# Scheduling priority for VectorE's operations of a state chain, and the distances 8, 10, 8 within a chunk

## The chip, the core and the metric

The kernel runs on one core of one Trainium2 chip. The metric is the device time of one execution in microseconds (us), the median of several runs. Five engines work side by side, each through its own queue in order: TensorE (PE: matmuls; PEld is its weight load), VectorE (DVE), ScalarE (ACT), GpSimd (POOL) and SyncE (SP, which only issues DMAs here).

## What is computed

A decoder block over 512 tokens of width 2048: a sliding-window attention branch and a gated DeltaNet branch from one normalised input, merged by gates, a projection and a last norm. The change touches the recurrence of the second branch, which runs over 8 chunks of 64 tokens for each of 32 value heads:

```
def step(state, inp):
    q_i, k_i, u_i, w_i, g_i, qk_i = inp
    v_new = u_i - w_i @ state
    o = (q_i * exp(g_i)) @ state + qk_i @ v_new
    k_dec = k_i * exp(g_last - g_i)
    state = state * exp(g_last) + k_dec^T @ v_new
    return state, o
```

## The kernel before

All matrix products with weights are done in float32 accuracy by splitting each operand into a rounded high part and the rest: `proj` takes two halves of a weight tile, and for each half `mm_half` gives PE eight matmuls high by high (L174), eight high by low (L176) and eight low by high (L179), 128x512 each. So a projection has 48 such matmuls. ACT makes the high part of a weight (L162); in the stage of the change GpSimd makes the low part (L165, two operations of 128x512 for each half).

PE's order is written out by the program. Everything else that PE must do is a generator (a job) in a `Flow`. After each matmul of a projection, `flow.tick()` counts all waiting jobs down by one, and a job that is due puts its next PE instructions at this place. `yield n` therefore means: n projection matmuls later. The orders on DVE, ACT and GpSimd are made by a scheduler, which takes among the operations that are ready, by its own account of time, the one of the best priority. Priority is by default the order of the program. Each engine then runs its list strictly in order.

In the stage of the change one head kh of 16 (a key head with its two value heads, h = 0 and 1) takes four projections, 192 matmuls: two value tiles and two gate tiles. After heads 3, 7 and 11 (`GATE_KH`) a fifth projection is put in, and at the end of the stage four more stand. Beside these run, as jobs: the causal convolution of a value tile (`conv`: three DVE operations L297 on the tile cy, after one on ACT), its transposes to tokens (`to_tokens`, vb, L538 and L539), the preparation of the keys of the next head (`prepare`: transposes L519, ktl by L523 and L525), the scan of a head (`scan`), and the output of a head (`finish`: L608 sums squares, eleven small operations L610 and L193 to L197 on 128x8 make a reciprocal root by Newton steps, L612 scales the whole output by it).

The scan is a serial chain through PE and DVE. For a chunk c it has four links:

- X (L555): PE multiplies the state `sn`; DVE makes `rr` of it (L561, one for each h), ACT makes xq.
- Y (L573): PE multiplies `rr`, DVE makes `sv` in three operations (L576 on both h, then L579 for each h), and `o` (L582), which isn't in the chain.
- SU (L588, L589): PE multiplies `sv`.
- DVE makes the new state `sn` (L594, one for each h; for the first chunk the copy L597, here called the seed).

The distances in matmuls are X to Y 8, Y to SU 8, SU to the next X 10. In the first chunk, which has no X, Y follows its start by 4. The scans of the heads stand in a queue of their own (`scans`), one behind the other; a scan of 8 chunks takes 194 matmuls.

Of the kernel before, what the change touches and what calls it, by code (L numbers as in the profile page):

```python
# [8 lines left out]
F32 = mybir.dt.float32  # L9
# [3 lines left out]
ALU = mybir.AluOpType  # L13
AX = mybir.AxisListType

P = 128
# [63 lines left out]
def hybrid_block(  # L80
# [21 lines left out]
    pe, dve, act, pool = nc.tensor, nc.vector, nc.scalar, nc.gpsimd  # L102
# [16 lines left out]
    def bank(tag, bufs=1):  # L119
        return ps.tile([P, S], F32, name=tag, bufs=bufs)  # L120
# [95 lines left out]
    eSuf = cst.tile([P, NT, 32], F32, name="eSuf")  # L216
    nbeG = cst.tile([P, NT, 32], F32, name="nbeG")
    vbe = cst.tile([P, NT, 32], F32, name="vbe")
    cq = cst.tile([P, NT, NK], F32, name="cq")
    eTot = [cst.tile([P, NT, 32], F32, name=f"eTot{p}") for p in range(2)]  # L220
# [265 lines left out]
    with ExitStack() as st:  # L486
# [58 lines left out]
        def scan(kh, vb, zs):  # L545
            slab, tq, kth, ktl = got.pop(kh)
            o = pv.tile([P, NT, 2, P], F32, name="o")
            s_cur = None
            v2 = slice(2 * kh, 2 * kh + 2)
            for c in range(8):  # L550
                T, p = divmod(c, 2)
                rk, rq = (H0, H1) if p == 0 else (H1, H0)
                if c:
                    xp = bank("pa").rearrange("p (h e) -> p h e", h=4)[:, 0:2, :]
                    pe.matmul(xp, slab[:, T, 2 * p:2 * p + 2, :].rearrange("d b i -> d (b i)"), s_cur,  # L555
                              start=True, stop=True)
                    rr = rrs[p]
                    xq = pv.tile([P, 2, P], F32, name="xq")
                    for h in range(2):
                        vh = 2 * kh + h  # L560
                        dve.scalar_tensor_tensor(rr[rk, h, :], xp[rk, h, :], nbeG[rk, T, vh:vh + 1], vb[rk, T, h, :],  # L561
                                                 ALU.mult, ALU.add)
                    for h in range(2):
                        vh = 2 * kh + h
                        act.activation(xq[rq, h, :], xp[rq, h, :], AF.Copy, scale=eGs[rq, T, vh:vh + 1])  # L565
                    yield 8
                else:
                    rr = rrs[p]
                    act.copy(rr[rk], vb[rk, T])
                    yield 4  # L570
                yp = bank("pb").rearrange("p (h e) -> p h e", h=4)[:, 0:2, :]
                for h in range(2):
                    pe.matmul(yp[:, h, :], tq[:, h * 4 + T, :], rr[:, h, :], start=True, stop=True)  # L573
                if c < 7:
                    sv = pv.tile([P, 2, P], F32R, name="sv")
                    dve.tensor_tensor(sv[rk], yp[rk], eSuf[rk, T, v2].unsqueeze(2).broadcast_to([64, 2, P]), ALU.mult)  # L576
                    for h in range(2):
                        vh = 2 * kh + h
                        dve.scalar_tensor_tensor(sv[rq, h, :], yp[rk, h, :], eSuf[rk, T, vh:vh + 1],  # L579
                                                 sv[rk, h, :].bitcast(F32), ALU.mult, ALU.subtract)  # L580
                if c:
                    dve.tensor_tensor(o[rq, T], xq[rq], yp[rq], ALU.add)  # L582
                else:
                    act.copy(o[rq, T], yp[rq])
                yield 8
                if c < 7:
                    su = bank("pc").rearrange("p (h e) -> p h e", h=4)[:, 0:2, :]
                    pe.matmul(su, kth[:, T, p, :], sv, start=True, stop=False)  # L588
                    pe.matmul(su, ktl[:, T, p, :], sv, start=False, stop=True)  # L589
                    s_new = pv.tile([P, 2, P], F32, name="sn")  # L590
                    if c:
                        for h in range(2):
                            vh = 2 * kh + h
                            dve.scalar_tensor_tensor(s_new[:, h, :], s_cur[:, h, :], eTot[p][:, T, vh:vh + 1],  # L594
                                                     su[:, h, :], ALU.mult, ALU.add)
                    else:
                        dve.tensor_copy(s_new, su)  # L597
                    s_cur = s_new
                    yield 10
            flow.start(finish(kh, o, zs))  # L600

        def finish(kh, o, zs):
            osq = pv.tile([P, NT * 2, P], F32, name="osq", bufs=1)
            ov = o.rearrange("p t h e -> p (t h) e")
            act.activation(osq, ov, AF.Square)
            so = pv.tile([P, 8], F32, name="so")
            ro = pv.tile([P, 8], F32, name="ro")
            dve.tensor_reduce(so, osq, AX.X, ALU.add)  # L608
            so4 = so.rearrange("p (t h) -> p t h", h=2)
            dve.scalar_tensor_tensor(so4, so4, 1.0 / P, cq[:, :, kh:kh + 1].broadcast_to([P, NT, 2]), ALU.mult, ALU.add)  # L610
            rsqrt(pv, ro, so, 8)
            dve.tensor_tensor(ov, ov, ro.unsqueeze(2).broadcast_to([P, 8, P]), ALU.mult)  # L612
            yield 36
            for h in range(2):
                tp = bank("tr", 2)
                for T in range(NT):
                    pe.transpose(tp[:, T * P:(T + 1) * P], o[:, T, h, :], ident)
                od = pv.tile([P, S], F32, name="od")
                tv = tp.rearrange("p (t c i) -> p t c i", t=NT, c=2)
                dv = od.rearrange("p (t c i) -> p t c i", t=NT, c=2)  # L620
                zv = zs[:, h, :].rearrange("p (t c i) -> p t c i", t=NT, c=2)
                for p in range(2):
                    dve.scalar_tensor_tensor(dv[:, :, p, :], tv[:, :, 1 - p, :], dnw, zv[:, :, p, :], ALU.mult, ALU.mult)
                nc.sync.dma_start(od_d[KT + 2 * kh + h], od)
                yield 6
# [4 lines left out]
        for kh in range(NK):  # L630
            vb = pv.tile([P, NT, 2, P], F32, name="vb")
            zs = pv.tile([P, 2, S], F32, name="zs", bufs=3)
            flow.start(prepare(kh), 24 if kh else 60)
            for h in range(2):
                vh = 2 * kh + h

                def then(acc):
                    y = conv(acc, 32 + vh, pv)
                    act.activation(y, y, AF.Silu)
                    after = (lambda kh=kh, vb=vb, zs=zs: scans.add(scan(kh, vb, zs))) if h else None  # L640
                    flow.start(to_tokens(y, vb, h, vh, after))

                proj(w_in[T_DN + 32 + vh], then)
            for h in range(2):
                proj(w_in[T_DZ + 2 * kh + h], lambda acc: act.activation(zs[:, h, :], acc, AF.Silu))
                if h == 0 and kh + 1 < NK:
                    load_head(kh + 1)
            if kh in GATE_KH:
                gate_tile(pv, 47 - n_gate)
                n_gate += 1  # L650
# [339 lines left out]
```

## Time and profile before

| what | value |
|---|---|
| median of 3 runs | 2933.49 us (2932.84 to 2934.3) |
| the profiled execution | 2932.62 us |
| its span in the profile | 2930.8 us |
| granted TensorE clock over the span | 0.997 of full speed |
| PE busy | 2848.7 us, 97% |
| DVE busy | 1766.8 us, 60% |
| ACT busy | 1028.7 us, 35% |
| GpSimd busy | 552.4 us, 19% |

Busy time is the time in which an engine has an instruction under way. The stage of the change lies between about 850 and 1850 us of the span. In a row of the timeline the first number is the start in us from the beginning of the span, the second the duration, x4 means that four equal instructions are merged, and the bracket at the end is the time that the engine stood idle before the instruction and what ended it.

### The profile page before, as it was taken

How to read it: one execution, taken by the hardware profiler on the slowest of the kernel's cores; microseconds unless marked ns; L12 is line 12 of the kernel's file. 1: busy time of each engine (PE TensorE's matmuls, PEld its weight loads, DVE VectorE, ACT ScalarE, POOL GpSimd, SP SyncE). 2: the span in 40 equal slices, each digit the busy share in tenths (PEclk: the TensorE clock that was granted, in tenths of full speed). 3: DMA queues.
4: the chain of work that ended last, by engine and by line, in shares of the span. 5: the costliest groups of instructions: out<-in, count | busy, mean ns of one | idle time of the engine just before them, and what ended most of it. 6: DMA issues, size and time to landing. Idle time of an engine off the chain costs nothing.

```text
span 2930.8 us, 36770 instructions
## 1 busy us (share of the span) xinstructions
PE 2848.7 (97%) x13594; PEld 2367.1 (81%) x13594; DVE 1766.8 (60%) x3520; ACT 1028.7 (35%) x1645; POOL 552.4 (19%) x464
## 2 busy tenths in 40 slices
PE   7999999999999999999999999999999999999998
PEld 7778888888887787788778778887788888888887
DVE  6686667979725555555555554378884455455434
ACT  5532222232333333334333333355553222222222
POOL 2410000000043333333333333023340000000010
PEclk9999999999999999999999999999999999999999
DMA  3344444353543333333333332423336554554533
GB/s 139 107 130 143 130 136 157 120 203 124 185 133 99 96 112 104 98 98 114 96 102 115 98 89 91 132 86 110 101 108 216 172 176 155 165 161 147 181 99 103
DMA packets 184627, 376.07 MB, mean 128 GB/s; under 512 B 65504, under 2 KB 82272, under 8 KB 183040
## 3 DMA queue, kind: packets, MB, share of 16 engines
q1 hardware_dynamic: 184448, 373.72, 40.7%
q8 instruction: 108, 1.77, 0.3%
q14 instruction: 71, 0.58, 0.1%
HBM read 316.97 MB, written 54.59 MB: 127 GB/s over the span
## 4 chain that ended last, share of the span: by engine, by line
PE 86%; DVE 10%; ACT 2%; issue 1%; POOL 0%; DMA 0%; SPq 0%; ACTq 0%; DVEq 0%
PE acc L179 24%; PE acc L176 23%; PE acc L174 23%; PE pa L555 2%; DVE cy L297 2%; PE pb L573 1%; PE fo L898 1%; PE fo L896 1%; PE fo L897 1%; PE acc L247 1%; PE tr L529 1%; DVE sv L579 1%; DVE ptl L760 1%; PE pc L588 1%; DVE ad L381 1%
## 5 line engine op out<-in xcount | busy, mean ns | idle before, releaser
L174 PE MATMUL acc<-hT_hi,whi 128*128 128x512 f32 x2592 | 1037.5, 400 | 0.0
L176 PE MATMUL acc<-hT_lo,whi 128*128 128x512 f32 x2592 | 1018.6, 393 | 0.0
L162 ACT CAST whi<-w 128x1024 fp32r<-128x1024 f32 x446 | 468.3, 1051 | 1183.4 <-PE acc L176 949.4
L179 PE MATMUL acc<-hT_hi,wlo 128*128 128x512 f32 x2592 | 685.6, 398 | 2.3 <-DVE wlo L165 2.3
L165 POOL TENSOR_TENSOR wlo<-w,whi 128x512 fp32r<-128x512 f32 x284 | 359.9, 1288 | 1283.6 <-PE acc L179 648.8
L165 DVE TENSOR_TENSOR wlo<-w,whi 128x512 fp32r<-128x512 f32 x608 | 423.3, 719 | 264.4 <-ACT whi L162 202.1
L176 PEld LDWEIGHTS acc<-hT_lo,whi 128*128 128x128 f32 x2592 | 488.7, 189 | 92.1
L174 PEld LDWEIGHTS acc<-hT_hi,whi 128*128 128x128 f32 x2592 | 488.4, 188 | 92.1
L179 PEld LDWEIGHTS acc<-hT_hi,wlo 128*128 128x128 f32 x2592 | 480.3, 188 | 99.0 <-DVE wlo L165 3.1
L174 PE MATMUL acc<-dh,whi 128*128 128x512 f32 x768 | 298.8, 389 | 0.0
L176 PE MATMUL acc<-dl,whi 128*128 128x512 f32 x768 | 298.8, 389 | 0.0
L179 PE MATMUL acc<-dh,wlo 128*128 128x512 f32 x768 | 189.7, 389 | 0.0
L561 DVE SCALAR_TENSOR_TENSOR rr<-pa,nbeG,vb 64x128 f32<-64x128 f32 x224 | 69.2, 348 | 183.8 <-PE pa L555 183.2
L297 DVE SCALAR_TENSOR_TENSOR cy<-acc,cw,cy 128x511 f32<-128x511 f32 (+2 forms) x192 | 142.8, 744 | 58.7 <-ACT cy L295 55.8
L859 DVE TENSOR_TENSOR gd<-acc,gl 128x512 f32<-128x512 f32 x80 | 55.2, 690 | 188.3 <-PE acc L179 188.3
L176 PEld LDWEIGHTS acc<-dl,whi 128*128 128x128 f32 x768 | 144.2, 188 | 30.0
L179 PEld LDWEIGHTS acc<-dh,wlo 128*128 128x128 f32 x768 | 144.1, 188 | 29.9
L174 PEld LDWEIGHTS acc<-dh,whi 128*128 128x128 f32 x768 | 144.1, 188 | 29.9
L916 POOL TENSOR_TENSOR y<-y,fw 128x512 f32<-128x512 f32 x12 | 18.9, 1609 | 658.7 <-ACT sqy L914 658.7
L576 DVE TENSOR_TENSOR sv<-pb,eSuf 64x256 fp32r<-64x256 f32 x112 | 46.9, 419 | 137.5 <-PE pb L573 137.3
L565 ACT ACTIVATE xq<-pa,eGs 64x128 f32<-64x128 f32 x224 | 69.0, 356 | 160.0 <-DVE rr L561 159.4
L467 DVE TENSOR_TENSOR m<-m,tm 128x62 f32<-128x62 f32 (+30 forms) x124 | 106.3, 857 | 2.8
(264 smaller groups left out, 3180.3 us busy)
## 6 DMA issues: line engine op xcount, KB each, us to landing
w<-w_in SPq DMA_DIRECT2D x326, 512.0 KB, 3.5
w<-w_dn SPq DMA_DIRECT2D x64, 512.0 KB, 3.5
gl<-ga_d SPq DMA_DIRECT2D x96, 256.0 KB, 2.6
w<-w_att SPq DMA_DIRECT2D x32, 512.0 KB, 3.9
w<-w_out SPq DMA_DIRECT2D x32, 512.0 KB, 3.5
of<-od_d SPq DMA_DIRECT2D x48, 256.0 KB, 4.0
kq_d<-slab SPq DMA_DIRECT2D x16, 512.0 KB, 2.8
ga_d<-gt SPq DMA_DIRECT2D x32, 256.0 KB, 3.0
```

Source lines behind the costliest of these rows:

```text
L162: act.copy(hi, w)
L165: lo_eng[0].tensor_sub(lo[:, r], w[:, r], hi[:, r].bitcast(F32))
L174: pe.matmul(acc, hi[:, k, :], rhi[k], start=first and k == 0, stop=False)
L176: pe.matmul(acc, hi[:, k, :], rlo[k], start=False, stop=False)
L179: pe.matmul(acc, lo[:, k, :], rhi[k], start=False, stop=last and k == n - 1)
L297: dve.scalar_tensor_tensor(y[:, sh:], acc[:, 0:S - sh], cw[:, t, 3 - sh:4 - sh], y[:, sh:], ALU.mult, ALU.add)
L467: dve.tensor_tensor(m[:, 0:jj, jj + 1:], m[:, 0:jj, jj + 1:], tm, ALU.add)
L555: pe.matmul(xp, slab[:, T, 2 * p:2 * p + 2, :].rearrange("d b i -> d (b i)"), s_cur, start=True, stop=True)
L561: dve.scalar_tensor_tensor(rr[rk, h, :], xp[rk, h, :], nbeG[rk, T, vh:vh + 1], vb[rk, T, h, :], ALU.mult, ALU.add)
L565: act.activation(xq[rq, h, :], xp[rq, h, :], AF.Copy, scale=eGs[rq, T, vh:vh + 1])
L576: dve.tensor_tensor(sv[rk], yp[rk], eSuf[rk, T, v2].unsqueeze(2).broadcast_to([64, 2, P]), ALU.mult)
L859: dve.tensor_tensor(gd, acc, gl, ALU.mult)
```

## The change

Three groups of DVE operations of the chain, those that make `rr`, `sv` and `sn`, are put into `with tc.high_priority()`: where one of them and another operation are ready together in the scheduler's account, the one of the chain is taken first. No operation is added or removed. The distances become X to Y 8, Y to SU 10, SU to X 8. The period of a chunk stays at 26 matmuls; in the last chunk, which has no SU, the end of the scan moves from 8 to 10 matmuls behind Y, so that a scan takes 196.

```
-                    for h in range(2):
-                        vh = 2 * kh + h
-                        dve.scalar_tensor_tensor(rr[rk, h, :], xp[rk, h, :], nbeG[rk, T, vh:vh + 1], vb[rk, T, h, :],
-                                                 ALU.mult, ALU.add)
+                    with tc.high_priority():
+                        for h in range(2):
+                            vh = 2 * kh + h
+                            dve.scalar_tensor_tensor(rr[rk, h, :], xp[rk, h, :], nbeG[rk, T, vh:vh + 1],
+                                                     vb[rk, T, h, :], ALU.mult, ALU.add)
...
-                    dve.tensor_tensor(sv[rk], yp[rk], eSuf[rk, T, v2].unsqueeze(2).broadcast_to([64, 2, P]), ALU.mult)
-                    for h in range(2):
-                        vh = 2 * kh + h
-                        dve.scalar_tensor_tensor(sv[rq, h, :], yp[rk, h, :], eSuf[rk, T, vh:vh + 1],
-                                                 sv[rk, h, :].bitcast(F32), ALU.mult, ALU.subtract)
+                    with tc.high_priority():
+                        dve.tensor_tensor(sv[rk], yp[rk], eSuf[rk, T, v2].unsqueeze(2).broadcast_to([64, 2, P]),
+                                          ALU.mult)
+                        for h in range(2):
...
-                yield 8
+                yield 10
                 if c < 7:
...
+                    with tc.high_priority():
+                        if c:
+                            for h in range(2):
...
+                        else:
+                            dve.tensor_copy(s_new, su)
                     s_cur = s_new
-                    yield 10
+                    yield 8
```

Three places of DVE's list show what this moves. The first is chunk 6 of head 4, where a convolution (cy) falls on the chain. Before:

```order
L561 SCALAR_TENSOR_TENSOR rr_6246<-pa,nbeG,vb 64x128 x2
L297 SCALAR_TENSOR_TENSOR cy<-acc,cw,cy 128x511
L576 TENSOR_TENSOR sv<-pb,eSuf 64x256
L297 SCALAR_TENSOR_TENSOR cy<-acc,cw,cy 128x510
L579 SCALAR_TENSOR_TENSOR sv<-pb,eSuf,sv 64x128
L297 SCALAR_TENSOR_TENSOR cy<-acc,cw,cy 128x509
L579 SCALAR_TENSOR_TENSOR sv<-pb,eSuf,sv 64x128
L582 TENSOR_TENSOR o<-xq,pb 64x256
```

The same place after the change (line numbers there are a little higher: L562 is rr, L578 and L582 are sv, L585 is o, L598 is sn):

```order
L562 SCALAR_TENSOR_TENSOR rr_6246<-pa,nbeG,vb 64x128 x2
L297 SCALAR_TENSOR_TENSOR cy<-acc,cw,cy 128x511
L578 TENSOR_TENSOR sv<-pb,eSuf 64x256
L297 SCALAR_TENSOR_TENSOR cy<-acc,cw,cy 128x510
L582 SCALAR_TENSOR_TENSOR sv<-pb,eSuf,sv 64x128 x2
L297 SCALAR_TENSOR_TENSOR cy<-acc,cw,cy 128x509
L598 SCALAR_TENSOR_TENSOR sn<-sn,eTot_100,pc 128x128 x2
L585 TENSOR_TENSOR o<-xq,pb 64x256
```

The two halves of sv now stand together; the third convolution has gone behind them, and one stays between L578 and L582.

The second place is the seed of head 6, from its sv on. Before, with the Newton steps (ro, nrt) and the scaling L612 of head 5's output around it:

```order
L579 SCALAR_TENSOR_TENSOR sv<-pb,eSuf,sv 64x128
L195 SCALAR_TENSOR_TENSOR nrt<-ro,so 128x8
L196 TENSOR_TENSOR nrt<-nrt,ro 128x8
L197 SCALAR_TENSOR_TENSOR ro<-nrt,ro 128x8
L195 SCALAR_TENSOR_TENSOR nrt<-ro,so 128x8
L196 TENSOR_TENSOR nrt<-nrt,ro 128x8
L597 COPY sn<-pc 128x256
L197 SCALAR_TENSOR_TENSOR ro<-nrt,ro 128x8
L612 TENSOR_TENSOR o<-o,ro 128x1024
```

The same place after (L616 is the scaling, L601 the seed):

```order
L582 SCALAR_TENSOR_TENSOR sv<-pb,eSuf,sv 64x128 x2
L196 TENSOR_TENSOR nrt<-nrt,ro 128x8
L197 SCALAR_TENSOR_TENSOR ro<-nrt,ro 128x8
L195 SCALAR_TENSOR_TENSOR nrt<-ro,so 128x8
L196 TENSOR_TENSOR nrt<-nrt,ro 128x8
L197 SCALAR_TENSOR_TENSOR ro<-nrt,ro 128x8
L616 TENSOR_TENSOR o<-o,ro 128x1024
L601 COPY sn<-pc 128x256
```

The seed has gone behind the last Newton step and the scaling. It is the same in head 7; in head 5 it stood behind the scaling before, too, and has two Newton steps between sv and the scaling now where there were three.

The third place is chunk 3 of head 6, where the keys of head 7 are prepared (ktl). Before:

```order
L576 TENSOR_TENSOR sv<-pb,eSuf 64x256
L579 SCALAR_TENSOR_TENSOR sv<-pb,eSuf,sv 64x128 x2
L582 TENSOR_TENSOR o<-xq,pb 64x256
L523 TENSOR_TENSOR ktl<-tr,kth 64x4x128
L525 CAST ktl<-ktl 64x4x128
L594 SCALAR_TENSOR_TENSOR sn<-sn,eTot_101,pc 128x128 x2
```

The same place after:

```order
L523 TENSOR_TENSOR ktl<-tr,kth 64x4x128
L525 CAST ktl<-ktl 64x4x128
L578 TENSOR_TENSOR sv<-pb,eSuf 64x256
L523 TENSOR_TENSOR ktl<-tr,kth 64x4x128
L582 SCALAR_TENSOR_TENSOR sv<-pb,eSuf,sv 64x128 x2
L585 TENSOR_TENSOR o<-xq,pb 64x256
```

Two operations of ktl now stand ahead of sv and one inside it. On PE the scan of head 6 stands 4 matmuls later than before, since the two scans ahead of it in the queue take 2 matmuls more each; so the four transposes L519, which stood right behind Y of this chunk, now stand four matmuls ahead of it.

## Rows read from the trace of the kernel before

**Rows 1.** Waits of PE, whole span: us in total, times, longest.
```profile
PE pc L588 <- DVE sv L579: 28.3, 27, 1.6
...
PE pa L555 <- DVE sn L597: 8.5, 8, 1.6
```
**Rows 2.** Waits of PE from 1098 to 1346 us, heads 4 to 7.
```profile
PE pc L588 <- DVE sv L579: 7.2, 7, 1.4
PE pa L555 <- DVE sn L597: 2.1, 2, 1.5
```
**Rows 3.** Timeline of PE, chunk 1 of head 4: Y, SU, X.
```profile
1112.26 0.61 PE L573 MATMUL pb<-rr,tq 128*128 128x128 f32 x4
...
1114.56 0.28 PE L588 MATMUL pc<-sv,kth 128*128 128x256 f32 x1
...
1117.07 0.59 PE L555 MATMUL pa<-sn,slabv 128*128 128x256 f32 x2
```
**Rows 4.** Timeline of DVE, the same chunk: sv, sn.
```profile
1112.91 0.43 DVE L576 TENSOR_TENSOR sv<-pb,eSuf 64x256 fp32r<-64x256 f32 x1 [1.67 <-PE pb L573]
1113.37 0.63 DVE L579 SCALAR_TENSOR_TENSOR sv<-pb,eSuf,sv 64x128 fp32r<-64x128 f32 x2
...
1114.99 0.61 DVE L594 SCALAR_TENSOR_TENSOR sn<-sn,eTot,pc 128x128 f32<-128x128 f32 x2 [0.55 <-PE pc L589]
```
**Rows 5.** Timeline of DVE, chunk 6 of head 4: convolution and sv.
```profile
1150.92 0.75 DVE L297 SCALAR_TENSOR_TENSOR cy<-acc,cw,cy 128x511 f32<-128x511 f32 x1 [1.51 <-ACT cy L295]
1151.59 0.40 DVE L576 TENSOR_TENSOR sv<-pb,eSuf 64x256 fp32r<-64x256 f32 x1
...
1152.68 0.34 DVE L579 SCALAR_TENSOR_TENSOR sv<-pb,eSuf,sv 64x128 fp32r<-64x128 f32 x1
...
1153.84 0.34 DVE L579 SCALAR_TENSOR_TENSOR sv<-pb,eSuf,sv 64x128 fp32r<-64x128 f32 x1
```
**Rows 6.** Timeline of PE, SU of this chunk.
```profile
1154.33 0.35 PE L588 MATMUL pc<-sv,kth 128*128 128x256 f32 x1 [1.41 <-DVE sv L579]
```
**Rows 7.** Timeline of DVE, head 5: Newton steps, scaling, seed.
```profile
1165.47 1.25 DVE L196 TENSOR_TENSOR nrt<-nrt,ro 128x8 f32<-128x8 f32 x1
...
1168.01 1.23 DVE L612 TENSOR_TENSOR o<-o,ro 128x1024 f32<-128x1024 f32 x1
1169.15 0.42 DVE L597 COPY sn<-pc 128x256 f32<-128x256 f32 x1
```
**Rows 8.** Timeline of PE, first X of head 5.
```profile
1169.62 0.70 PE L555 MATMUL pa<-sn,slabv 128*128 128x256 f32 x2 [1.54 <-DVE sn L597]
```
**Rows 9.** Timeline of GpSimd at this place.
```profile
1165.41 2.53 POOL L165 TENSOR_TENSOR wlo<-w,whi 128x512 fp32r<-128x512 f32 x2 [3.75 <-issue]
```
**Rows 10.** Timeline of DVE, head 6: a Newton step with GpSimd idle.
```profile
1229.30 0.17 DVE L197 SCALAR_TENSOR_TENSOR ro<-nrt,ro 128x8 f32<-128x8 f32 x1
```
**Rows 11.** Timeline of GpSimd, head 6.
```profile
1226.70 2.54 POOL L165 TENSOR_TENSOR wlo<-w,whi 128x512 fp32r<-128x512 f32 x2 [3.45 <-issue]
```
**Rows 12.** Timeline of PE, first X of head 6.
```profile
1230.25 0.70 PE L555 MATMUL pa<-sn,slabv 128*128 128x256 f32 x2 [0.57 <-DVE sn L597]
```
**Rows 13.** Timeline of PE, chunk 3 of head 6: Y and the keys' transposes.
```profile
1247.74 0.61 PE L573 MATMUL pb<-rr,tq 128*128 128x128 f32 x4
1248.19 0.60 PE L519 MATMUL tr<-ident,kc 128*128 128x128 f32 x4
```
**Rows 14.** Timeline of ACT there.
```profile
1248.82 0.58 ACT L522 CAST kth<-tr 64x512 fp32r<-64x512 f32 x1 [1.40 <-PE tr L519]
```
**Rows 15.** Timeline of GpSimd there.
```profile
1248.04 2.54 POOL L165 TENSOR_TENSOR wlo<-w,whi 128x512 fp32r<-128x512 f32 x2 [3.66 <-ACT xq L565]
```
**Rows 16.** Timeline of DVE, chunk 5 of head 7: ktl.
```profile
1322.52 0.68 DVE L523 TENSOR_TENSOR ktl<-tr,kth 64x512 fp32r<-64x512 f32 x1 [1.21 <-ACT kth L522]
1323.23 0.81 DVE L525 CAST ktl<-ktl 64x512 fp32r<-64x512 f32 x1
```
**Rows 17.** Timeline of GpSimd there.
```profile
1321.24 2.52 POOL L165 TENSOR_TENSOR wlo<-w,whi 128x512 fp32r<-128x512 f32 x2 [4.10 <-issue]
```

More of the change, by code (lines that the diff above doesn't have):

```diff
@@ L575, in scan @@
                     sv = pv.tile([P, 2, P], F32R, name="sv")
-                    dve.tensor_tensor(sv[rk], yp[rk], eSuf[rk, T, v2].unsqueeze(2).broadcast_to([64, 2, P]), ALU.mult)
-                    for h in range(2):
-                        vh = 2 * kh + h
-                        dve.scalar_tensor_tensor(sv[rq, h, :], yp[rk, h, :], eSuf[rk, T, vh:vh + 1],
-                                                 sv[rk, h, :].bitcast(F32), ALU.mult, ALU.subtract)
+                    with tc.high_priority():
+                        dve.tensor_tensor(sv[rk], yp[rk], eSuf[rk, T, v2].unsqueeze(2).broadcast_to([64, 2, P]),
+                                          ALU.mult)
+                        for h in range(2):
+                            vh = 2 * kh + h
+                            dve.scalar_tensor_tensor(sv[rq, h, :], yp[rk, h, :], eSuf[rk, T, vh:vh + 1],
+                                                     sv[rk, h, :].bitcast(F32), ALU.mult, ALU.subtract)
                 if c:
@@ L590, in scan @@
                     s_new = pv.tile([P, 2, P], F32, name="sn")
[L591 to L597, printed above, removed]
+                    with tc.high_priority():
+                        if c:
+                            for h in range(2):
+                                vh = 2 * kh + h
+                                dve.scalar_tensor_tensor(s_new[:, h, :], s_cur[:, h, :], eTot[p][:, T, vh:vh + 1],
+                                                         su[:, h, :], ALU.mult, ALU.add)
+                        else:
+                            dve.tensor_copy(s_new, su)
                     s_cur = s_new
-                    yield 10
+                    yield 8
             flow.start(finish(kh, o, zs))
```

## The prediction

> **What bounds the kernel now.** PE is busy for 97% of the span, in an order that the program writes out, and the change leaves the number of its matmuls as it is. So only time in which PE stands still can go or come. I read the waits of PE first. Over the whole span PE waits 28.3 us in 27 places at SU for sv and 8.5 us in 8 places at X for sn, 36.8 us together [rows 1]; these are the waits that the change can touch, and 36.8 us is the most that it can give. The same view by stretch says that they come back every four heads, the rhythm of the projection put in after heads 3, 7 and 11: heads 4 to 7 have 7.2 us in 7 places and 2.1 us in 2 [rows 2], 9.3 us, and four times this is 37.2 us (the last four heads have a little less). So I work out heads 4 to 7 and multiply.
>
> Then the timeline of a chunk with nothing else on DVE. Y starts at 1112.26, SU at 1114.56, X at 1117.07 [rows 3]; sv is ready at 1114.00 and sn at 1115.60 [rows 4]. SU starts 0.15 us after sv's end where it waits (1153.84 + 0.34, then 1154.33 [rows 5, 6]), so it could go at 1114.15: a slack of 0.41 us. For X the step is 0.05 us (1169.57, then 1169.62 [rows 7, 8]): it could go at 1115.65, a slack of 1.42 us. The lengths 2.30 us for 8 matmuls and 2.51 us for 10 give about 0.23 us for one, so two are 0.45 us. The link through sv is tight and waits when DVE does something else first; the link through sn waits only at the seed.
>
> **The distances.** Two matmuls more to SU, two less to X: slacks of 0.86 and 0.97 us in place of 0.41 and 1.42. Undisturbed chunks wait nowhere before and after. Where SU waits, 0.45 us goes. A scan takes 196 matmuls instead of 194 and a head has 192; so within four heads the second scan starts 2 later than now, the third 4, the fourth 6 (0.45, 0.91, 1.36 us), and the fifth projection takes it up again. At the end of the stage the last scan is 8 matmuls late, beside four projections of 48; this costs nothing, and without that cover 8 x 0.23 = 1.8 us.
>
> **The priority at the convolutions.** Chunk 6 of head 4: the first convolution is ready ahead of Y's result and stays first, L576 runs at 1151.59, the second convolution stays between, and the halves of sv then stand together. The first starts at 1152.68 as now, the two take 0.63 us [rows 4, 5], and sv ends at 1153.31, not 1154.18. SU may go at 1153.46; without its wait it would have come at 1154.33 - 1.41 = 1152.92 [rows 6] and now comes 0.45 us later, 1153.37. There remains 0.1 us of 1.41. The same addition for the four other places of this kind in heads 5 and 6, with their chains shifted, gives 0.1, 0.3 (two convolutions ahead of sv), 0 and 0.1 us. Together 0.6 us.
>
> **The priority at the keys.** In chunk 5 of head 7 ktl leaves sv free, and a wait goes whole. In chunk 3 of head 6 one comes. The transposes now start where Y started, 1247.74, and Y 0.45 us (the transposes' own time) and 0.91 us later, 1249.10 [rows 13]. ACT's copy starts 0.63 us behind the transposes and takes 0.58 [rows 13, 14], so L523 runs from 1248.95 to 1249.65. L525 then falls into GpSimd's pair of operations, which ends at 1250.58 [rows 15]. What that does is seen in head 7: there L525 took 0.81 us and ended at 1324.04, 0.28 us after GpSimd's pair (1323.76) [rows 16, 17]. So it ends at 1250.86, and behind it come L578 with 0.43, L523 with 0.69 and sv's halves with 0.63 us: 1252.6, SU at 1252.75. Due is 1249.10 + 2.30 + 0.45 = 1251.85. A new wait of 0.9 us.
>
> **The seeds.** Here the priority doesn't help. Head 5: after sv two Newton steps remain, and GpSimd's pair from 1165.41 to 1167.94 [rows 9] holds them: a step took 1.25 us inside the pair [rows 7], 0.17 us outside [rows 10]. The scaling starts at 1167.97, and X follows a scaling that stands ahead of the seed by 1169.62 - 1168.01 = 1.61 us [rows 7, 8]: 1169.58. Due is 1169.62 - 1.54 + 0.45 = 1168.53. The wait is 1.05 us in place of 1.54. Head 6: the pair ends at 1229.24 [rows 11] and holds two of five steps, three more take 0.2 us each with the gap, the scaling starts at 1229.9 and X at 1231.51; due is 1230.25 - 0.57 + 0.91 = 1230.59 [rows 12]. The wait is 0.9 us in place of 0.57. Head 7 has the same order; before, its wait was at SU, with a Newton step inside sv. I take 0.9 us. In head 4 the seed is free of Newton steps. Together 2.9 us.
>
> A rule bears on these two parts: the Trainium skill, "SBUF — State Buffer", section "SBUF: two separate sides", says that VectorE and GpSimd share a pair of SBUF ports as an exclusive lock, held for a whole instruction, and that the other side is blocked meanwhile. The trace agrees for L196 (1.25 against 0.17 us). By the rule the scaling, with two operands in SBUF, would be blocked too if it started inside a pair, which no run here shows; that makes a rival below.
>
> **The sum.** Heads 4 to 7 wait 0.6 + 0.9 + 2.9 = 4.4 us instead of 9.3. Four times 4.4 is 17.6 us against 36.8: 19.2 us go. The profiled execution took 2932.6 us, 0.9 us less than the median of the runs: 2913.4 us on its scale, 2914 us as a median. Everything else I take at nothing: no operation is added; ACT's copies for xq stand a place earlier or later between the casts of the weights, and in this stage the view of PE's waits names none for such a cast, only the two kinds of [rows 2].
>
> The bounds of what no row shows. GpSimd's pairs may stand elsewhere against the steps: without any overlap head 5's scaling would start at about 1166, and all seeds come in time (0 us); if each seed also waits for one more held step, 3 x 1.25 us come on top of 2.9. At the sv places the least is 0, and the most what they cost now, 6.2 us without the one that I count with head 7's seed. The new wait at the keys lies between 0 and 0.9 us. So four heads wait between 0 and 6.2 + 0.9 + 6.7 = 13.8 us, which is 2897 to 2952 us as a median, and I take 4.4, since each term comes from the row nearest to it.
>
> **Rivals.**
> - The waits go nearly whole: GpSimd's pairs slip past the Newton steps and the keys. For it: a held step depends on tenths of a us, and in the seed's neighbourhood the chain moves by 0.45 to 1.36 us. Against: GpSimd's place is tied to the projections, which keep theirs. What stays is about 1 us in four heads, 33 us go: 2900 us.
> - The waits only change places: chains shifted by 2, 4 and 6 matmuls meet other operations, as at the keys. Five more such waits of 0.9 us in four heads would eat the 4.9 us: 2932 us. Against it: in the new order nothing but one operation ever stands between the first and the other two operations of sv. For it: in two heads of four the seed has gone behind the scaling.
> - Slower: the scaling itself falls into GpSimd's pair and is held, with the seed and the whole chain behind it. The place is the seeds of the 12 heads that follow another without a fifth projection; the price is up to 2.5 us (a pair) each. The gain is gone from 19.2 / 12 = 1.6 us each on; at the full price 30 us come and 19 go: 2944 us. Against it: the Newton steps ahead of the scaling are held themselves until the pair ends, so that the scaling starts behind it [rows 7, 9].
> - The priority may not do what it says: at the seeds it doesn't, but at sv the order shows the halves together.
>
> **Chances.** The forecast 0.72, nearly whole 0.10, places changed 0.10, slower 0.06, something else 0.02. What a measurement of this kernel can tell from no change is about 0.2%, 5.9 us: faster means below 2927.6, which holds all of the first two and a little of the third; with its upper tail counted off, 0.84. Same 0.10, slower 0.06. The range: the forecast's own is 2.5 us to either side for four heads, 10 us in all, 2904 to 2924; to hold 8 in 10 with the rivals it reaches from 2902 to 2926.
>
> **What would show it.** SU's wait for sv falls from 28.3 us to about 6 to 10, most of it in two places of four heads (the keys in the third head, a seed); X's wait for the seed rises from 8.5 to about 11 or 12 us, in 12 places. L579's successor shows its two halves merged at the convolutions. DVE's busy time and PE's count of matmuls stay. I am wrong if the X waits are small (then GpSimd was elsewhere), if many new places of SU below 0.5 us appear, or if PE waits for casts of weights in the stage.

## The result and the profile after

| | us |
|---|---|
| predicted | 2914.0 (2902 to 2926) |
| after, median of 4 runs | 2914.12 (2912.18 to 2914.93) |
| before, beside it | 2933.32 (2932.84 to 2934.3) |
| ratio | 0.9933, 95% interval 0.9922 to 0.9945 |
| the profiled execution, span | 2914.18, 2912.4 |

The kernel became 19.2 us faster. The granted clock is 0.997 as before. The page's line of busy times is nearly that of before, so the time came out of PE's idle time. The two profiled executions differ by 18.4 us, which falls into two parts: from the first X to the end of the span 2069.4 us became 2048.5, 20.9 us less, while the first X started at 863.9 us instead of 861.4, 2.5 us later, after work that the change leaves alone.

```profile
PE 2850.0 (98%) x13594; PEld 2370.9 (81%) x13594; DVE 1762.9 (61%) x3520; ACT 1028.6 (35%) x1645; POOL 555.8 (19%) x464
```

The waits of PE over the whole span (us in total, times, longest), which answer to [rows 1]; L601 is the seed, L582 the halves of sv, L591 is SU:

```profile
PE pa L555 <- DVE sn L601: 13.2, 12, 1.5
...
PE pc L591 <- DVE sv L582: 4.2, 5, 1.2
```

28.3 + 8.5 = 36.8 us in 35 places became 13.2 + 4.2 = 17.4 us in 17. SU's wait for sv fell to a seventh, X's wait for the seed grew by a half. In heads 4 to 7 (1096 to 1342 us; [rows 2] before) the same view has 3.4 us in 3 places and 0.7 in one.

**The convolution.** VectorE's timeline in chunk 6 of head 4, which answers to [rows 5]: start, duration, operation, and in brackets the idle time before it.

```profile
1148.39 0.75 DVE L297 SCALAR_TENSOR_TENSOR cy<-acc,cw,cy 128x511 f32<-128x511 f32 x1 [1.50 <-ACT cy L295]
1149.06 0.40 DVE L578 TENSOR_TENSOR sv<-pb,eSuf 64x256 fp32r<-64x256 f32 x1
1149.39 0.73 DVE L297 SCALAR_TENSOR_TENSOR cy<-acc,cw,cy 128x510 f32<-128x510 f32 x1
1150.15 0.60 DVE L582 SCALAR_TENSOR_TENSOR sv<-pb,eSuf,sv 64x128 fp32r<-64x128 f32 x2
```

The halves of sv stand together and end at 1150.75; SU started at 1150.90 and had stood idle for 0.09 us by PE's records, in place of the 1.41 us of [rows 6].

**The keys.** Chunk 3 of head 6 on VectorE, on GpSimd and on PE ([rows 13 to 15] before):

```profile
1243.15 1.16 DVE L525 CAST ktl<-ktl 64x512 fp32r<-64x512 f32 x1
1244.34 0.43 DVE L578 TENSOR_TENSOR sv<-pb,eSuf 64x256 fp32r<-64x256 f32 x1
1244.69 0.69 DVE L523 TENSOR_TENSOR ktl<-tr,kth 64x512 fp32r<-64x512 f32 x1
1245.41 0.63 DVE L582 SCALAR_TENSOR_TENSOR sv<-pb,eSuf,sv 64x128 fp32r<-64x128 f32 x2
```
```profile
1241.48 2.54 POOL L165 TENSOR_TENSOR wlo<-w,whi 128x512 fp32r<-128x512 f32 x2 [4.09 <-issue]
```
```profile
1242.55 0.61 PE L574 MATMUL pb<-rr,tq 128*128 128x128 f32 x4
...
1245.05 0.39 PE L176 MATMUL acc<-hT_lo,whi 128*128 128x512 f32 x1
1246.18 0.35 PE L591 MATMUL pc<-sv,kth 128*128 128x256 f32 x1 [0.74 <-DVE sv L582]
```

The cast L525 lies across the end of GpSimd's pair (1244.02), takes 1.16 us and ends 0.29 us after it; all of sv stands behind it.

**The seed of head 5** on VectorE, GpSimd and PE, which answers to [rows 7 to 9]:

```profile
1161.48 0.17 DVE L196 TENSOR_TENSOR nrt<-nrt,ro 128x8 f32<-128x8 f32 x1
1161.68 1.17 DVE L197 SCALAR_TENSOR_TENSOR ro<-nrt,ro 128x8 f32<-128x8 f32 x1
1162.88 2.27 DVE L616 TENSOR_TENSOR o<-o,ro 128x1024 f32<-128x1024 f32 x1
1165.08 0.41 DVE L601 COPY sn<-pc 128x256 f32<-128x256 f32 x1
```
```profile
1161.53 2.54 POOL L165 TENSOR_TENSOR wlo<-w,whi 128x512 fp32r<-128x512 f32 x2 [3.76 <-issue]
```
```profile
1165.54 0.70 PE L555 MATMUL pa<-sn,slabv 128*128 128x256 f32 x2 [1.17 <-DVE sn L601]
```

Here is a thing that the trace of before doesn't have: the scaling L616 runs inside GpSimd's pair (1161.53 to 1164.07) and takes 2.27 us, not 1.23. In heads 6 and 7 it starts behind the pair; head 6 on VectorE and GpSimd:

```profile
1219.92 0.60 DVE L582 SCALAR_TENSOR_TENSOR sv<-pb,eSuf,sv 64x128 fp32r<-64x128 f32 x2
1220.55 0.60 DVE L196 TENSOR_TENSOR nrt<-nrt,ro 128x8 f32<-128x8 f32 x1
1221.18 1.22 DVE L197 SCALAR_TENSOR_TENSOR ro<-nrt,ro 128x8 f32<-128x8 f32 x1
...
1223.04 1.22 DVE L616 TENSOR_TENSOR o<-o,ro 128x1024 f32<-128x1024 f32 x1
```
```profile
1219.84 2.54 POOL L165 TENSOR_TENSOR wlo<-w,whi 128x512 fp32r<-128x512 f32 x2 [2.83 <-issue]
```

### The profile page after: what moved, and what is told of

The parts are those of the page before. It is cut to its first block, busy times and chain, and to the rows that moved or that the text cites. A ratio compares the mean times of both kernels' runs of the same rounds, so it can differ in the third digit from the quotient of the medians.

```text
span 2912.4 us, 36773 instructions
## 1 busy us (share of the span) xinstructions
PE 2850.0 (98%) x13594; PEld 2370.9 (81%) x13594; DVE 1762.9 (61%) x3520; ACT 1028.6 (35%) x1645; POOL 555.8 (19%) x464
## 4 chain that ended last, share of the span: by engine, by line
PE 88%; DVE 8%; ACT 2%; issue 1%; POOL 0%; DMA 0%; SPq 0%; ACTq 0%; DVEq 0%
PE acc L179 24%; PE acc L176 24%; PE acc L174 24%; PE pa L555 2%; PE pb L574 2%; PE fo L902 1%; PE fo L900 1%; PE fo L901 1%; PE acc L247 1%; PE tr L529 1%; DVE ptl L764 1%; DVE o L616 1%; DVE ro L197 1%; DVE wlo L165 1%; DVE ad L381 1%
## 5 line engine op out<-in xcount | busy, mean ns | idle before, releaser
L176 PE MATMUL acc<-hT_lo,whi 128*128 128x512 f32 x2592 | 1018.7, 393 | 0.0
L176 PEld LDWEIGHTS acc<-hT_lo,whi 128*128 128x128 f32 x2592 | 488.6, 188 | 92.8
L176 PE MATMUL acc<-dl,whi 128*128 128x512 f32 x768 | 298.8, 389 | 0.0
L176 PEld LDWEIGHTS acc<-dl,whi 128*128 128x128 f32 x768 | 144.2, 188 | 30.0
L562 DVE SCALAR_TENSOR_TENSOR rr<-pa,nbeG,vb 64x128 f32<-64x128 f32 x224 | 69.0, 348 | 143.2 <-PE pa L555 143.0
L578 DVE TENSOR_TENSOR sv<-pb,eSuf 64x256 fp32r<-64x256 f32 x112 | 46.9, 418 | 116.7 <-PE pb L574 116.4
```

What stands on the lines that cost most here:

```text
L176: pe.matmul(acc, hi[:, k, :], rlo[k], start=False, stop=False)
```

## The experiments

The theory after the result: two causes lie on one another. One is VectorE's own order around sv, which the change mends. The other is GpSimd's operations, which hold VectorE's small steps, its casts of the keys and its scaling; the change leaves that as it is, and it is all that still waits.

**The priority alone** (distances 8, 8, 10 as before):

```
-                yield 10
+                yield 8
...
-                    yield 8
+                    yield 10
```

> The priority with the distances of before (8, 8, 10). Theory A (the order on DVE costs most of the waits, the distances add 0.45 us each): in four heads the convolution places keep 0.5, 0.1, 0.5, 0.5 and 0.4 us, the keys in head 7 keep 0.7 (sv is split by ktl as before), the seeds keep 1.5, 0.4 and 0.4 us: 5.0 instead of 9.3 us, so about 2916 to 2918 us. Rival B (the distances do it, the priority little): 2928 to 2933 us.

Measured: 2917.66 us (2915.99 to 2918.28), ratio 0.9944, interval 0.9932 to 0.9957, theory A. X waits 11.2 us for the seed, in 12 places. Of PE's waits, SU for sv:

```profile
PE pc L591 <- DVE sv L582: 9.8, 19, 0.7
```

Without the two matmuls SU waits in 19 places, none over 0.7 us: an operation of 0.75 us inside sv goes past the 0.41 us of slack by a few tenths.

**The distances alone** (8, 10, 8, the `with` blocks taken out):

```
-                    with tc.high_priority():
-                        dve.tensor_tensor(sv[rk], yp[rk], eSuf[rk, T, v2].unsqueeze(2).broadcast_to([64, 2, P]),
-                                          ALU.mult)
+                    dve.tensor_tensor(sv[rk], yp[rk], eSuf[rk, T, v2].unsqueeze(2).broadcast_to([64, 2, P]), ALU.mult)
```

and so for rr and sn.

> The distances 8, 10, 8 without the priority. Theory A: sv stays split at two convolution places (1.0 us each left), rr is split twice (0.8 and 0.2 us, now as a wait of Y), the keys keep 0.7, the seeds 0 to 1.1, 0.9 and 1.3 us: 6.2 to 7.3 instead of 9.3 us, so 2922 to 2927 us. Rival B: 2914 to 2917 us. In head 5 the scaling of the output would start inside GpSimd's pair of operations: if the pair holds it too, the seed there waits 1.1 us, if not, nothing.

Measured: 2926.33 us (2924.26 to 2929.05), ratio 0.9977, interval 0.9968 to 0.9986, theory A. X waits 9.8 us in 11 places. Of PE's waits, SU for sv:

```profile
PE pc L588 <- DVE sv L579: 12.5, 15, 1.5
```

So the priority gives 16.0 us by itself, the distances 7.3, both together 19.2: they mend partly the same waits. The scaling L612 is held in this kernel, too, which answers the question that the expectation left open; with the priority alone it is held as well (there it is L616; shortest, median, longest in ns, first here, then there):

```profile
L612 DVE TENSOR_TENSOR o<-o,ro x16: 1224/1225/2273, 918.3 to 1835.2; 128x1024 f32<-128x1024 f32 x16
```
```profile
L616 DVE TENSOR_TENSOR o<-o,ro x16: 1224/1225/2274, 918.1 to 1825.1; 128x1024 f32<-128x1024 f32 x16
```

So either part of the change puts the scaling into a pair. At the seed of head 5 the sum of squares, from which the Newton steps start, stands 3.95 or 3.96 us ahead of GpSimd's pair in the kernel before and in all three others; but nine of the eleven small operations start ahead of the pair before the change, and ten with either part of it or both. The eleventh then waits for the first half of the pair and the scaling for the second.

**The scaling on ScalarE.** If it is VectorE's scaling that stands ahead of the seed, the seed must be free when ACT does it:

```
-            dve.tensor_tensor(ov, ov, ro.unsqueeze(2).broadcast_to([P, 8, P]), ALU.mult)
+            for i in range(8):
+                act.activation(ov[:, i, :], ov[:, i, :], AF.Copy, scale=ro[:, i:i + 1])
```

> The changed kernel with the scaling of a head's output as eight 128x128 operations on ACT instead of one on DVE, so that the seed comes right behind the last Newton step. Theory A (the seeds wait for held Newton steps and then 1.23 us of scaling, in series): the 13.2 us of waits at X go to 0 to 2 us: about 2901 us. Rival C (GpSimd's hold on the Newton steps alone makes the seeds late): half or more of the 13.2 us stays, 2908 us or more. Rival D (ACT's 2.9 us more per head delay xq or the casts of the weights): new waits of PE, no gain.

Measured: 2897.71 us (2897.4 to 2898.97), ratio 0.9878, interval 0.9865 to 0.9892. The line of L555 is gone from PE's waits; SU's stays:

```profile
PE pc L591 <- DVE sv L582: 4.1, 5, 1.2
```

16.4 us came out where the line was 13.2 us. The profiled executions differ by 16.8 us; 14.5 of it lies behind the first X (from there to the end of the span 2048.5 us became 2034.0), the rest ahead of it, where the edit changes nothing. The section on the hardware says why 13.2 us of recorded idle time can cost more.

**The keys' cast on ScalarE as well:**

```
-                dve.tensor_copy(ktl[r2, :, p, :], ktl[r, :, p, :].bitcast(F32))
+                act.copy(ktl[r2, :, p, :], ktl[r, :, p, :].bitcast(F32))
```

> As the kernel before it in this list, and the copy L525 of ktl to the other half on ACT as well, not on DVE. Theory A: the waits at the keys (0.74 us, four times) go too, since the operation that GpSimd's pair holds no longer stands ahead of sv: about 2898 us. Rival (the keys' wait comes from the extra operations ahead of sv, held or not): 0.3 us of each stays, 2900 us. Rival D as above.

Measured: 2894.79 us (2893.66 to 2896.69), ratio 0.9868, interval 0.9855 to 0.9882. The keys' waits are gone from the line; one of 0.3 us is new in it:

```profile
PE pc L591 <- DVE sv L582: 1.5, 2, 1.2
```

It went 3 us further down, as expected, though the intervals of the two ratios overlap. A wait of 0.6 us for ktl is new at the transposes L538.

**The priority on sv alone.** The blocks around rr and sn are made plain:

```
-                    with tc.high_priority():
+                    if True:
                         for h in range(2):
                             vh = 2 * kh + h
                             dve.scalar_tensor_tensor(rr[rk, h, :], xp[rk, h, :], nbeG[rk, T, vh:vh + 1],
```

> The changed kernel with the priority left on the operations of sv alone; rr and sn go back to the default. Theory A (the link through sn has 0.97 us to spare after the change, so that one convolution of 0.75 us inside sn or rr hides): the time stays at that of the changed kernel, 2913 to 2916 us, and PE's waits stay two lines, X for the seed about 13 us and SU for sv about 4 us. Rival B (the link through sn and rr needs the priority too, since sn and rr are now split by a convolution in some four places of every four heads): a new wait of 0.3 to 0.7 us in each, 16 places, so 2919 to 2925 us, with a line of X or Y behind sn (L595) or rr.

Measured: 2920.3 us (2915.81 to 2923.0), ratio 0.9955, interval 0.9942 to 0.9969: too wide to tell. So it ran again beside the changed kernel.

> The changed kernel as it is, timed beside the three others of this comparison. 2912 to 2916 us by every theory.

> The priority on sv alone, beside the changed kernel on the same chip, since the first runs of it spread from 2915.8 to 2923.0 us. Theory A (the priority of rr and sn is worth nothing): within 2 us of the changed kernel, 2913 to 2917 us. Rival B (it is worth something in most executions): 4 us or more above the changed kernel, 2918 to 2923 us, with PE waits behind rr or sn in the profile.

Measured: the changed kernel 2914.36 us (2911.66 to 2914.85), ratio 0.9932 (0.992 to 0.9945); with the priority on sv alone 2918.66 us (2917.71 to 2920.44), ratio 0.9949 (0.9936 to 0.9963). The size is rival B's, its reason isn't: no wait behind a split rr or sn of VectorE appeared. What the changed kernel doesn't have are these two lines:

```profile
PE tr L621 <- DVE o L616: 3.4, 3, 1.8
...
PE pb L574 <- ACT rr L570: 1.0, 3, 0.3
```

The first is the output of every fourth head, which waits for its scaling. The longest is at 1346 us, and it is again GpSimd. Its timeline there, with its copy of the keys behind a load and four low parts in one stretch:

```profile
1338.84 0.63 POOL L511 COPY kc<-slabv 128x512 f32<-128x512 f32 x1 [7.18 <-DMA slabv<-kq_d]
1339.42 5.05 POOL L165 TENSOR_TENSOR wlo<-w,whi 128x512 fp32r<-128x512 f32 x4
```

The Newton steps of head 7 meet this stretch, and three of them, one behind the other, take 1.2 us each; the first:

```profile
1340.78 1.21 DVE L195 SCALAR_TENSOR_TENSOR nrt<-ro,so 128x8 f32<-128x8 f32 x1
```

In the changed kernel a pair has ended at 1337.4 there, and the next starts at 1339.8 with the scaling. Why the load of the keys lands later here wasn't tried and stays open. The distances alone show the same: there this copy has up to 7.2 us of idle time ahead of it, and PE waits 2.4 us for the scaling in two places; with the priority alone, as in the kernel before, the copy has at most 1.9 us ahead of it and PE has no such wait.

**GpSimd idle in the stage.** The low parts of the weights stay on VectorE, two more operations for each half of a weight; GpSimd keeps only its copy of the keys, 0.6 us once for each head:

```
         scans = Queue(flow)
-        lo_eng[0] = pool
         load_head(0)
```

> The changed kernel with the low parts of the weights (L165) made by VectorE in this stage too, so that GpSimd has no work there. Theory A (VectorE's long Newton steps, its casts of the keys' low parts and its long scaling are held by GpSimd's operations): no Newton step takes over 0.3 us, every scaling L616 takes 1.22 us and none 2.27, and L525 takes 0.42 us everywhere. Rival B (the long durations belong to VectorE's own operations, by a reader or writer of the same tile): steps of 1.2 us and a scaling of 2.27 us are still there. The time is of less weight: VectorE gets two operations of about 0.65 us for each half of a weight, about a third of the stage's VectorE time more, and the seeds lose their cover or gain it; 2890 to 2925 us by either theory.

Measured in this single run: 2887.7 us; then timed, beside the same edit in the kernel before:

> The changed kernel with the low parts on VectorE, so that GpSimd is idle in the stage; its one run took 2887.7 us, with no wait of PE in the stage. Theory A: that holds, 2886 to 2890 us. Rival B: one favourable run, the median lies at 2893 us or above.

> The kernel before (no priority, distances 8, 8, 10) with the low parts on VectorE in this stage. Theory A (two independent causes: VectorE's own order around sv, which the change mends, and GpSimd's holds, which it doesn't): the seeds and keys wait nowhere, but SU still waits for sv where two convolutions (2 x 0.75 us against 0.41 us of slack, 1.1 us in some 4 places of four heads) or an operation of the low parts (0.69 against 0.41, 0.3 us in some 7 places) stand between its operations: 6.5 us in four heads, 26 in the stage, against 36.8 now, so 2918 to 2924 us. Rival B (GpSimd's holds are the whole matter, and with them gone the old order does as well): 2887 to 2893 us.

Measured: in the changed kernel 2889.06 us (2888.07 to 2889.82), ratio 0.9847, interval 0.9834 to 0.9861. In the kernel before 2936.45 us (2935.09 to 2938.31), ratio 1.001, interval 1.0001 to 1.0018. First the changed kernel's groups on VectorE from 860 us to the last X (busy time, mean ns), with GpSimd at work:

```profile
L616 DVE TENSOR_TENSOR o<-o,ro 128x1024 f32<-128x1024 f32 x15 | 22.6, 1504 | 0.5
L525 DVE CAST ktl<-ktl 64x512 fp32r<-64x512 f32 x30 | 20.8, 692 | 0.9
L197 DVE SCALAR_TENSOR_TENSOR ro<-nrt,ro 128x8 f32<-128x8 f32 x45 | 18.9, 419 | 1.5
```

and with GpSimd idle:

```profile
L165 DVE TENSOR_TENSOR wlo<-w,whi 128x512 fp32r<-128x512 f32 x268 | 179.5, 688 | 54.4 <-ACT xq L566 21.6 <-issue 21.6 <-ACT cy L642 7.0
L616 DVE TENSOR_TENSOR o<-o,ro 128x1024 f32<-128x1024 f32 x15 | 18.3, 1220 | 0.3
L525 DVE CAST ktl<-ktl 64x512 fp32r<-64x512 f32 x30 | 12.7, 422 | 1.0
L197 DVE SCALAR_TENSOR_TENSOR ro<-nrt,ro 128x8 f32<-128x8 f32 x45 | 7.4, 165 | 1.3
```

The scaling falls from 1504 to 1220 ns, the cast from 692 to 422, the step from 419 to 165: the hold is GpSimd's, theory A. The edit does two things at once, though: it takes the hold away and gives VectorE more work, so that its gain isn't the price of the hold alone. VectorE has 180 us of low parts more, and PE never waits in the stage. Its busy time from 1096 to 1342 us (PE, PEld, DVE, ACT, POOL) in the changed kernel and in this one:

```profile
1096.00:1342.00 246.00, 241.77 (x1216) 201.55 (x1215) 138.33 (x348) 93.63 (x155) 89.94 (x73) 1.00 0.34 106
```
```profile
1096.00:1342.00 246.00, 246.00 (x1243) 206.56 (x1243) 174.77 (x417) 94.20 (x158) 2.93 (x4) 1.00 0.35 108
```

In the old order the same edit gives nothing. The X waits are gone, and SU's grow:

```profile
PE pc L588 <- DVE sv L579: 34.6, 38, 2.0
```

One of its longest is chunk 6 of head 4 again, where low parts of weights and convolutions stand around the parts of sv:

```profile
1153.40 1.29 DVE L165 TENSOR_TENSOR wlo<-w,whi 128x512 fp32r<-128x512 f32 x2 [0.85 <-ACT xq L565]
1154.61 0.74 DVE L297 SCALAR_TENSOR_TENSOR cy<-acc,cw,cy 128x511 f32<-128x511 f32 x1
1155.27 0.41 DVE L576 TENSOR_TENSOR sv<-pb,eSuf 64x256 fp32r<-64x256 f32 x1
1155.60 0.73 DVE L297 SCALAR_TENSOR_TENSOR cy<-acc,cw,cy 128x510 f32<-128x510 f32 x1
1156.36 0.34 DVE L579 SCALAR_TENSOR_TENSOR sv<-pb,eSuf,sv 64x128 fp32r<-64x128 f32 x1
```

I had expected 2918 to 2924 here and missed by 12 us: I gave an operation of the low parts 0.3 us each, and 1.1 us to the two convolutions inside sv, but did not count that two operations of the low parts and a convolution come ahead of it, too (1153.40 to 1155.27). That is read at this one place; the 38 places were not added up one by one. That there are two causes stands: the X waits are gone in both orders, and the edit is worth nothing in the old order and 25.3 us behind the change. That they add up independently, as theory A had it, isn't shown, since in the old order the low parts make waits of their own. The changed kernel with the low parts on VectorE is the fastest version of this study, 44 us below the kernel before.

## Why the prediction was right

The time is right, 2914.0 against 2914.1 us, and so is the sum, 17.6 us of waits against 17.4. Both are closer than the working deserves. The signs came out less well: SU's wait is 4.2 us where 6 to 10 were forecast, X's 13.2 where 11 or 12 were, in the 12 places forecast. By its steps, for heads 4 to 7:

- **The bound.** That PE's waits decide is shown: with no wait left in the stage the time is 2889 us. That 36.8 us is the most that can be had was wrong; the recorded idle time is less than a wait costs, and 44 us were there. For the same reason 19.4 us less of recorded waits gave back 20.9 us, not 19.4; the 2.5 us by which the first X is late in this execution hid it.
- **The distances.** 0.45 us for SU was right: an undisturbed SU comes 2.76 us behind Y (1267.24 to 1270.00) instead of 2.30, and the priority alone leaves 19 waits, with the distances 5. The 0.23 us for one matmul is right, too, though 2.30 and 2.51 us don't give it as they stand: the first holds Y's own 0.37 us, the second SU's 0.23.
- **The convolutions**, predicted 0.6 us, left 0.1: 0.09 us at chunk 6 of head 4 (predicted 0.1), 0.04 at chunk 4 of head 5, nothing at the others. The term is over by 0.5 us, 0.3 of it at the place with two convolutions ahead of sv (chunk 6 of head 5): SU starts there 2.83 us behind Y, 0.08 late, which the record doesn't show as idle time. Why it isn't 0.3 wasn't followed up.
- **The keys**, predicted 0.9 us, measured 0.74. Each step came as worked out: the cast ends 0.29 us after the pair (0.28 predicted), sv's end stands 1.73 us behind that (1.74). SU came 1246.18 - 1242.55 = 3.63 us after Y, where 2.75 were due: 0.9 late. The record shows 0.74, since it counts idle time from the end of the matmul before.
- **The seeds**, predicted 1.05 + 0.9 + 0.9, measured 1.17 + 1.07 + 1.13 = 3.4 us. Here the mechanism was only half right. In heads 6 and 7 it is the one predicted: two steps held, three short, the scaling behind the pair; in head 6 the pair stands 0.15 us later against X's due time, and head 7 was taken over from it. In head 5 I had both remaining steps held and the scaling behind the pair. In fact one step slipped in ahead, the next was held by GpSimd's first operation, and the scaling by its second. It ends at 1165.15, 1.08 us behind the pair's end; behind the pair it would have ended at 1164.07 + 0.03 + 1.22 = 1165.3. So the price is nearly the same, since the hold ends with the pair, whichever operation it is: the pair stands 0.29 us later against X's due time, the held scaling ends 0.17 us sooner, and 1.05 became 1.17 us.
- **The last head** has a wait of SU of 1.2 us, two small operations held ahead of sv; I had worked out only heads 4 to 7 and multiplied.
- **The rivals.** The mechanism of the slower one came true in four heads, and its price didn't: I had put a whole pair on top of the steps that are held ahead, where the scaling takes the place of one of them in it. The argument against it, that the steps ahead are held until the pair ends, failed in these heads, where ten of the eleven small operations are started when the pair begins. The Trainium skill, "SBUF — State Buffer", section "SBUF: two separate sides", says what it would do, a shared pair of ports locked for a whole instruction; 2.27 against 1.22 us, and 1.22 everywhere with GpSimd idle, agree with it. Waits that change places were not seen beyond the keys and that last head.
- **The priority doesn't help the seeds:** right, 8.5 us became 13.2 (11.2 with the priority alone). What does is to free VectorE of the scaling (16.4 us) or of GpSimd (25.3 us).

That the numbers meet is in part luck. The excess of the seeds (0.5 us) and the lack at the convolutions (0.5 us) cancel, and so do the higher price of a wait and the late first X; the forecast was not as sharp as the 0.1 us looks.

## What to carry to other kernels

When an engine is late by tenths of a microsecond, look for operations of the same kind and shape with two durations, and lay the other engines' timelines beside the long ones: 0.17 and 1.2 us for one step told of GpSimd. An engine that takes work off another may cost the kernel more than it spares: 180 us of low parts came back to VectorE here and the kernel became 25 us faster, but only with an order in which the chain goes first. So test two causes of one wait together as well as one by one: the low parts' edit was worth nothing alone.

## What the runs showed of the hardware

- A small held operation of VectorE ends with one of GpSimd's operations: L197 of head 6 at 1222.40, the pair at 1222.38. A larger one ends later, the cast L525 0.29 us behind the pair and the scaling 1.08 us. In the stage of the changed kernel the 11 casts L525 that start inside a low part on GpSimd take 1152 to 1164 ns, the 19 others 420 to 424. The halves of sv, which read PSUM, go through at their usual length: 52 of them lie wholly inside a low part and take 332 to 355 ns, the 172 others 332 to 358.
- The hold goes the other way, too. Where the scaling starts a little ahead of a pair, in the changed kernel's second profile at 1339.77, it takes its 1.22 us, and the pair takes 3.59 us instead of 2.54:

```profile
1339.77 1.22 DVE L616 TENSOR_TENSOR o<-o,ro 128x1024 f32<-128x1024 f32 x1
```
```profile
1339.79 3.59 POOL L165 TENSOR_TENSOR wlo<-w,whi 128x512 fp32r<-128x512 f32 x2 [2.41 <-ACT whi L162]
```

- A wait costs more than its recorded idle time. The matmuls of 128x512 start every 0.23 us and are recorded with 0.39; a late one loses 0.16 us before idle time begins. SU undisturbed, in the kernel with GpSimd idle:

```profile
1153.27 0.39 PE L176 MATMUL acc<-hT_lo,whi 128*128 128x512 f32 x1
1153.49 0.28 PE L591 MATMUL pc<-sv,kth 128*128 128x256 f32 x1
```

- At the keys it started 1.13 us after L176, with an idle time of 0.74: 0.91 us late by the 0.22 above, and it then took 0.35 in place of 0.28. By the first and last start of X (count, then shortest, median, longest in ns, then the two starts), the changed kernel and that one with GpSimd idle take

```profile
L555 PE MATMUL pa<-sn,slabv x224: 376/377/483, 863.9 to 1815.2; 128*128 128x256 f32 x112
```
```profile
L555 PE MATMUL pa<-sn,slabv x224: 377/377/382, 861.5 to 1789.0; 128*128 128x256 f32 x112
```

951.3 and 927.5 us for the same matmuls: 23.8 us for 17.4 us of recorded waits. Laid side by side by the starts of X, Y and SU, 21.6 of the 23.8 us arise at the 17 places with a recorded wait, and the rest at other places of the chain, 0.2 us or less each.
